# HGRN2's values projected 512 features wide and kept in the residual's place, in a four-layer trunk on one core

## The chip, the cores and the metric

The kernel runs on 1 core of one Trainium2 chip. Time is device microseconds of one launch on that core. The kernel before takes 2690.08 us, the median of 3 runs (2689.09 to 2697.81).

## The reference

The reference sends 1024 positions of 1024 features, in f32, through four layers. Each layer is `x = x + gate * mixer(rmsnorm(x, norm_g) * (1 + scale) + shift)`, with shift, scale and gate from a conditioning vector, and every mixer ends in `(o * silu(z)) @ w_out`. Layers 0 and 3 are HGRN2, layer 1 is sliding-window attention, layer 2 is gated DeltaNet. Cut to what the change touches, they are:

```python
# HGRN2, 8 heads of 128, chunks of 64 (layers 0 and 3)
q, f_pre, i_, z = split(h @ w_in, 4)          # i_ holds the values, 1024 features
f = lb + (1 - lb) * sigmoid(f_pre);  k = (1 - lb) * sigmoid(-f_pre);  q = silu(q)
A = einsum('bhtd,bhsd,bhtsd->bhts', q_, k_, dec)
o = A @ v_ + (q_ * exp(b)) @ S                # then S is carried on
o = rmsnorm(o, onorm_g);  y = (o * silu(z)) @ w_out

# sliding-window attention, 16 query heads on 4 key heads of 64 (layer 1)
q = rope(rmsnorm(q)); k = rope(rmsnorm(k)); p = softmax(s with a learned sink); o = p @ v

# gated DeltaNet, 16 value heads of 128, chunks of 64 (layer 2)
q, k, v = split(silu(causal_conv(qkv, conv_w)))     # then l2norm of q and k
X = triangular_solve(A + eye, rhs)                  # A is 64x64, strictly lower
```

## The kernel before, in words

**Tiling and stages.** The residual x lies in SBUF as two halves of 512 positions (`x[0]`, `x[1]`, 2 MB each, two slots with the tag "x"), features on the partitions. The normed input of a layer lies beside it, split into a high and a low part (`hhi`, `hlo`, four slots with the tag "h"). Every projection product is a triple on TensorE: high by high, low by high, high by low (`mm3`, L201 to L206). The weights of a projection are loaded as f32 (`w_raw`, three buffers), rounded on ScalarE (`w_hi`, L179) and subtracted on VectorE (`w_lo`, L180) by `load_w`.

There are two kinds of input projection. `proj_fm` (L509) puts the features on the partitions and streams 512 positions in one product. `proj_tm` (L1170) puts the positions on the partitions and streams 256 features: HGRN2's values, and the queries, keys and values of the attention layer. In HGRN2 it is called by `proj_v(m)` (L1013), once for each pair of heads, and the values of the pair go to a buffer `hg_v`.

**HGRN2** (L956). `mix(h, d)` (L1026) computes the scores of one head by levels of a tree over the chunk. At level 5 a burst of small products (L1087), 96, 64 and 32 columns wide, fills three partition strips of `lev_ps`. After that come the state, the products with the values, the norm, four transposes on TensorE into `ot_ps` (L1136), the product with the gate `hg_zs` on VectorE (L1139) and a DMA to DRAM (`od`, L1141). The output projection reads `od` back as `o_in` (L1192). Heads 0 to 6 go that way; head 7 stays in SBUF.

**DeltaNet** (L537). `conv` (L636) is a causal convolution: two reads of PSUM on ScalarE (`gd_xs` L644, `gd_tb` L648), three multiply-adds on VectorE (L650), a Tanh. `inverse` (L732) inverts the 64x64 blocks in four steps, each a burst of small products into `z_ps` (L811 to L836) with copies behind it. `norm_apply` (L496) makes hhi and hlo, by way of a buffer `n_t`, eight pieces for each half.

**What sets the order.** Every engine runs its instructions in the order that a scheduler gave them, from priorities. `weave` (L68) interleaves streams of work by the costs that they yield. `early` (L114) raises a projection's start, `burst` (L134) and `tied` (L138) keep the small products of one step together. All DMAs named here are issued by SyncE (SP), on one queue. `spill_x` and `fill_x` (L125, L129) send a half of x to DRAM and bring it back. Before the change that happens in layers 1 and 2 alone.

## Time and profile before

| what | value |
|---|---|
| median of 3 runs | 2690.08 us (2689.09 to 2697.81) |
| the profiled execution's own time | 2695.95 us |
| its span, first to last instruction | 2694.2 us |
| granted TensorE clock, mean | 0.992 |
| TensorE products busy | 2609.7 us, 97% |
| VectorE busy | 2010.2 us, 75% |
| ScalarE busy | 1272.9 us, 47% |
| GpSimd busy | 136.7 us, 5% |

The first row is the measure; the others come from one execution that was profiled. "Busy" is the union of an engine's instructions in time. Products follow one another before the last has ended, so the modelled length of one product (0.39 us for 512 columns) is longer than the step from one start to the next; it is the steps that add up to the span. The granted clock is a share of full speed: 1.0 is 2.4 GHz, 0.5 is 1.2 GHz. The first projection product of layer 0 starts at 55 us; layer 0 ends near 631 us, layer 1 near 1112, layer 2 near 2110, layer 3 at the end.

### The profile page before, as it was taken

The page shows a single profiled execution, that of the slowest core. Times are in us where ns is not written, and L with a number is a line of the kernel's source. Part 1 is how long each engine was busy: PE and PEld are TensorE (multiplying, and loading weights), DVE is VectorE, ACT ScalarE, POOL GpSimd, SP SyncE. Part 2 cuts the span into 40 slices and gives each one's busy share as a digit, 9 for nine tenths or more (in the row PEclk, how much of TensorE's full clock was granted, in tenths as well). Part 3 has the DMA queues.
Part 4 walks back from the last instruction along what each step waited for, and adds up shares of the span by engine and source line. Part 5 has one row for each costly group of instructions (what it writes and reads, how often), then busy time and mean ns, then how long its engine had stood idle before and what let it go on. Part 6 is the DMA issues. An engine that isn't in the chain of part 4 may idle for free.

```text
span 2694.2 us, 51458 instructions
## 1 busy us (share of the span) xinstructions
PE 2609.7 (97%) x18927; PEld 2102.4 (78%) x18927; DVE 2010.2 (75%) x5619; ACT 1272.9 (47%) x3268; POOL 136.7 (5%) x352
## 2 busy tenths in 40 slices
PE   8999999999999999999999999999999999999998
PEld 4878878778878777677877777777788878787877
DVE  6776766788687877777988888989876766656575
ACT  4333333444454655454556556666644433333342
POOL 0000100000000000001001101100000000000000
PEclk9999999999999999999999999999999999999999
DMA  6332222344223252333343333333584221111133
GB/s 241 92 93 84 68 79 72 110 137 157 59 87 103 75 158 91 114 98 84 102 115 99 96 105 100 94 97 82 179 254 132 71 60 37 56 51 43 49 118 115
DMA packets 361490, 273.29 MB, mean 101 GB/s; under 512 B 70499, under 2 KB 294166, under 8 KB 361238
## 3 DMA queue, kind: packets, MB, share of 16 engines
q1 hardware_dynamic: 360950, 268.96, 33.9%
q8 instruction: 149, 2.44, 0.4%
q14 instruction: 103, 0.84, 0.1%
q0 software_dynamic: 288, 1.05, 0.1%
HBM read 224.77 MB, written 45.15 MB: 100 GB/s over the span
## 4 chain that ended last, share of the span: by engine, by line
PE 71%; DVE 17%; DMA 5%; ACT 3%; issue 3%; SPq 1%; POOL 0%; DVEq 0%; ACTq 0%; POOLq 0%
PE proj_ps L206 10%; PE proj_ps L205 9%; PE proj_ps L204 9%; PE outp_ps L204 5%; PE outp_ps L205 5%; PE outp_ps L206 5%; DMA ada_w<-in_ada_w_dram 3%; PE projt_ps L204 3%; PE projt_ps L206 3%; PE projt_ps L205 3%; DVE w_lo L180 2%; DVE gd_tb L650 2%; PE pv_ps L1374 1%; DVE ada_acc L413 1%; PE w_ps L890 1%
## 5 line engine op out<-in xcount | busy, mean ns | idle before, releaser
L204 PE MATMUL proj_ps<-hhi,w_hi 128*128 128x512 f32 x1664 | 675.8, 406 | 6.1 <-ACT gd_tb L648 5.9
L206 PE MATMUL proj_ps<-hhi,w_lo 128*128 128x512 f32 x1664 | 679.9, 409 | 0.0
L205 PE MATMUL proj_ps<-hlo,w_hi 128*128 128x512 f32 x1664 | 671.2, 403 | 0.0
L204 PEld LDWEIGHTS proj_ps<-hhi,w_hi 128*128 128x128 f32 x1664 | 315.3, 190 | 59.4 <-ACT gd_tb L648 6.3
L205 PEld LDWEIGHTS proj_ps<-hlo,w_hi 128*128 128x128 f32 x1664 | 314.7, 189 | 59.0 <-issue 2.4
L206 PEld LDWEIGHTS proj_ps<-hhi,w_lo 128*128 128x128 f32 x1664 | 315.0, 189 | 56.1 <-issue 1.0
L179 ACT CAST w_hi<-w_raw 128x512 fp32r<-128x512 f32 x332 | 202.0, 611 | 303.3 <-PE proj_ps L205 188.1
L180 DVE TENSOR_TENSOR w_lo<-w_raw,w_hi 128x512 fp32r<-128x512 f32 x332 | 223.1, 674 | 155.2 <-ACT w_hi L179 129.1
L205 PE MATMUL projt_ps<-w_lo,hhi 128*128 128x256 f32 x896 | 258.7, 291 | 4.7 <-DVE w_lo L180 4.7
L204 PE MATMUL projt_ps<-w_hi,hhi 128*128 128x256 f32 x896 | 257.8, 290 | 0.6 <-ACT w_hi L179 0.6
L206 PE MATMUL projt_ps<-w_hi,hlo 128*128 128x256 f32 x896 | 256.8, 290 | 0.0
L204 PE MATMUL outp_ps<-o_hi,w_hi 128*128 128x512 f32 x576 | 229.2, 400 | 4.7 <-ACT o_hi L1200 3.4
L205 PE MATMUL outp_ps<-o_lo,w_hi 128*128 128x512 f32 x576 | 229.4, 399 | 0.0
L206 PE MATMUL outp_ps<-o_hi,w_lo 128*128 128x512 f32 x576 | 226.8, 396 | 0.7 <-DVE w_lo L183 0.7
L205 PEld LDWEIGHTS projt_ps<-w_lo,hhi 128*128 128x128 f32 x896 | 171.1, 192 | 8.1 <-DVE w_lo L180 6.0
L204 PEld LDWEIGHTS projt_ps<-w_hi,hhi 128*128 128x128 f32 x896 | 171.1, 192 | 3.7 <-ACT w_hi L179 1.0
L206 PEld LDWEIGHTS projt_ps<-w_hi,hlo 128*128 128x128 f32 x896 | 170.8, 192 | 2.4 <-issue 1.0
L650 DVE SCALAR_TENSOR_TENSOR gd_tb<-gd_xs,taps,gd_tb 128x512 f32<-128x512 f32 x192 | 145.2, 756 | 28.3 <-ACT gd_tb L648 19.7
L182 ACT ACTIVATE w_hi<-w_raw,par 128x512 fp32r<-128x512 f32 (+1 forms) x136 | 94.3, 698 | 137.0 <-PE outp_ps L205 89.2
L204 PEld LDWEIGHTS outp_ps<-o_hi,w_hi 128*128 128x128 f32 x576 | 108.8, 189 | 29.1 <-ACT o_hi L1200 4.9
L413 DVE SCALAR_TENSOR_TENSOR ada_acc<-ada_w,par,ada_acc 128x512 f32<-128x512 f32 x140 | 104.8, 749 | 33.4 <-DMA ada_w<-in_ada_w_dram 32.5
L206 PEld LDWEIGHTS outp_ps<-o_hi,w_lo 128*128 128x128 f32 x576 | 108.7, 189 | 23.5 <-DVE w_lo L183 1.3
(398 smaller groups left out, 4894.8 us busy)
## 6 DMA issues: line engine op xcount, KB each, us to landing
ada_w<-in_ada_w_dram SPq DMA_DIRECT2D x160, 256.0 KB, 2.8
w_raw<-in_hg_in_w_dram SPq DMA_DIRECT2D x136, 256.0 KB, 2.8
w_raw<-in_gd_in_w_dram SPq DMA_DIRECT2D x108, 256.0 KB, 3.0
o_in<-od SPq DMA_DIRECT2D x72, 256.0 KB, 3.2
w_raw<-in_gd_out_w_dram SPq DMA_DIRECT2D x64, 256.0 KB, 2.9
w_raw<-in_sw_in_w_dram SPq DMA_DIRECT2D x48, 256.0 KB, 2.9
w_raw<-in_hg_out_w_dram SPq DMA_DIRECT2D x40, 256.0 KB, 2.8
ada_w<-in_ada_w_dram SPq DMA_DIRECT2D x8, 1024.0 KB, 9.2
```

What stands on the lines that cost most here:

```text
L179: nc.scalar.copy(hi, raw)
L180: nc.vector.tensor_tensor(lo, raw, hi.bitcast(F32), ALU.subtract)
L182: nc.scalar.activation(hi, raw, AF.Copy, scale=scale)
L204: mm(out, a[0], b[0], start=start, stop=False)
L205: mm(out, a[0], b[1], start=False, stop=False)
L206: mm(out, a[1], b[0], start=False, stop=stop)
L413: self.nc.vector.scalar_tensor_tensor(acc, w, c, acc, ALU.mult, ALU.add)
L650: nc.vector.scalar_tensor_tensor(y, xs[:, j:j + HT], w(j), y, ALU.mult, ALU.add)
L890: nc.tensor.matmul(po[:, hd[a]], dd["u"][a, hf][:, cs], rhs, start=True, stop=True)
L1374: nc.tensor.matmul(po[a * 64:(a + 1) * 64], vg[:, n + 1 - nkb + b, :], p4[:, :, a, :], start=b == 0, stop=b == nkb - 1)
```

## The change

1. **Values.** `proj_wide` and `load_wide` project HGRN2's values 512 features wide, for four heads at a time, into `projw_ps`. The values lie in the two "x" slots (`hg_v`), those of head 7 in two small tiles. x goes to DRAM before both HGRN2 layers and comes back ahead of their output projection.
2. **HGRN2's output.** For heads 0 to 6 the four TensorE transposes are replaced by one 32x32-block transpose on VectorE and four DMAs of 64 KB to a new DRAM tile `pd`; `gate()` reads it back in the next half's level 3, multiplies by the gate and stores to `od`.
3. **Level 5.** The burst has 16 products at most 64 columns wide on four strips, and is tied; one more copy on ScalarE.
4. **DeltaNet's inverse.** The bursts into `z_ps` are issued behind the final product of the triple that was written last (`apart`), with larger yields; `ZL` hands the gate projections out in halves, so their weights are loaded twice.
5. **The norm of the second half** is a generator. In DeltaNet its pieces are issued between the convolutions of the first half, and the projection starts with k, q and three z of the first half. `n_t` lies in PSUM.
6. **Attention.** v and q of the first half come first, k of all positions after; k's reciprocal root is taken for two tiles at once; the products with the values are tied behind both transposes.
7. **The stored output** uses an "h" slot in place of a pool of its own.

```diff
-ZL = ((2, 0, 1),), ((3, 0, 1),), ((4, 0, 1),), ((5, 0, 1),), ((6, 0),), ((6, 1),), ((7, 0, 1),), ()
+ZL = ((2, 1), (3, 0)), ((3, 1), (4, 0)), ((4, 1), (5, 0)), ((5, 1), (6, 0)), ((6, 1),), ((7, 0),), ((7, 1),), ()
...
+    def apart(self, mms):
+
+        with self.tc.issue_after(self.mm.ins):
+            self.tied(mms)
...
+    def load_wide(self, w, c0, pool):
+
+        return [self.load_w(w[:, k, c0:c0 + HT], None, (None, pool)[k % 2]) for k in range(KT)]
+
...
-            t = self.np.tile([P, HT], F32, name="n_t", tag="n_t", bufs=NB["n_t"])
+            t = self.psum("lev", "n_t", 2)
             G, S = self.gcol[:, i, k:k + 1], self.shift(i, k)
             nc.vector.scalar_tensor_tensor(t, x[:, k, :], G, rb, ALU.mult, ALU.mult)
-            nc.scalar.activation(hhi[:, k, :], t, AF.Identity, bias=S)
+            self.piece = nc.scalar.activation(hhi[:, k, :], t, AF.Identity, bias=S)
             nc.vector.scalar_tensor_tensor(hlo[:, k, :], t, S, hhi[:, k, :].bitcast(F32), ALU.add, ALU.subtract)
+            yield 1
...
-            nc.scalar.copy(xs[:, 3:], ps)
+            with self.tc.issue_after(self.hold.ins) if self.hold else nullcontext():
+                nc.scalar.copy(xs[:, 3:], ps)
...
-                nc.vector.scalar_tensor_tensor(y, xs[:, j:j + HT], w(j), y, ALU.mult, ALU.add)
+                last = nc.vector.scalar_tensor_tensor(y, xs[:, j:j + HT], w(j), y, ALU.mult, ALU.add)
+
+            self.piece = None
+            with self.tc.issue_after(last.ins):
+                drain(take(self.last, self.parts))
+            self.hold = self.piece
...
-            with self.burst():
-                for g in range(N):
-                    for z, p_, b_ in ((za, 0, 1), (zb, 2, 3)):
-                        nc.tensor.matmul(z[R[b_], g, :], uv[R[p_], g, R[b_]], Tc[R[p_], g, :], start=True, stop=True)
+            self.apart([lambda g=g, z=z, p_=p_, b_=b_: nc.tensor.matmul(z[R[b_], g, :], uv[R[p_], g, R[b_]], Tc[R[p_], g, :], start=True, stop=True)
+                        for g in range(N) for z, p_, b_ in ((za, 0, 1), (zb, 2, 3))])
...
-            yield 900
+            yield 2200
...
-        self.early(proj_kq(0, ds[0], ((0,),)), EV)
+        self.parts = 4
+        self.early(chain(proj_kq(0, ds[0], ((0,),)), proj_z(1, ds[1], (0,)), proj_z(2, ds[2], (0,))), EV)
+        drain(self.last)
         self.spill_x(1)
...
-                    ds[h]["v", hf] = v[:, :, (h % 2) * P:(h % 2 + 1) * P]
+
+        vs, v7 = [None, None], [mp.tile([P, NC, P], F32, name=f"hg_v7{n}") for n in range(2)]
+
+        def proj_v(m):
+
+
+            def ev(tt, ps):
+                hf, c = divmod(tt, NC)
+                if vs[hf] is None:
+                    vs[hf] = self.xslot("hg_v").rearrange("p (c a) n -> p c (a n)", a=2)
+                n = HT - m * P
+                nc.scalar.copy(vs[hf][:, c, m * HT:m * HT + n], ps[:, :n])
+                if m:
+                    nc.scalar.copy(v7[hf][:, c, :], ps[:, n:])
+
+            yield from self.proj_wide(self.load_wide(w_in, 2 * D + m * HT, mp), ev, range(2 * NC))
+
+        value = lambda h, hf: v7[hf] if h == H - 1 else vs[hf][:, :, h * P:(h + 1) * P]
+        v4 = lambda x, o: x.rearrange(f"p ({o} r) -> p c b r", c=NC, b=4)
+        pend = []
+
+        def gate():
+
+            h, hf, z = pend.pop()
+            rows = (slice(h * P, (h + 1) * P), slice(hf * HT, (hf + 1) * HT))
+            t = tl("tmp")
+            nc.sync.dma_start(t, self.pd[rows])
+            nc.vector.tensor_tensor(v4(z, "c b"), v4(t, "b c"), v4(z, "c b"), ALU.mult)
+            nc.sync.dma_start(od[rows], z)
...
-                        with self.burst():
-                          for c in range(NC):
-                            for g in range(3):
-                                gs = slice(g * 32, (g + 1) * 32)
-                                nc.tensor.matmul(pl[gs, c, g + 1:, :], kg[:, c * P + g * 32:c * P + (g + 1) * 32], xv[:, c, g::3 if g == 0 else 4 - g, :][:, :3 - g, :] if g < 2 else xv[:, c, 2:3, :], start=True, stop=True)
-                        for g in range(3):
-                            gs = slice(g * 32, (g + 1) * 32)
-                            nc.scalar.copy(at[gs, :, (g + 1) * 32:], pl[gs, :, g + 1:, :].rearrange("p c b t -> p c (b t)"))
+
+                        def mm(c, k, g, x, b):
+                            return nc.tensor.matmul(pl[g * 32:(g + 1) * 32, c, b], kg[:, c * P + k * 32:c * P + (k + 1) * 32], xv[:, c, x, :], start=True, stop=True)
+
+                        self.tied([lambda c=c, m=m: mm(c, *m) for c in range(NC) for m in (
+                            (0, 3, slice(6, 7), slice(3, 4)), (0, 0, slice(0, 4, 3), slice(1, 3)),
+                            (1, 1, slice(1, 5, 3), slice(2, 4)), (2, 2, slice(2, 3), slice(3, 4)))])
+                        for k, g, b0, b1 in ((0, 0, 1, 3), (1, 1, 2, 4), (2, 2, 3, 4), (0, 3, 3, 4)):
+                            nc.scalar.copy(at[k * 32:(k + 1) * 32, :, b0 * 32:b1 * 32], pl[g * 32:(g + 1) * 32, :, b0:b1, :].rearrange("p c b t -> p c (b t)"))
                         yield 900
+                    if l == 3 and pend:
+                        gate()
...
-                yield 436
-                of = tl("tmp")
-                nc.vector.tensor_tensor(of, pt, d["zs", hf], ALU.mult)
                 if h < HA:
-                    nc.sync.dma_start(od[h * P:(h + 1) * P, hf * HT:(hf + 1) * HT], of)
+
+
+                    nc.vector.tensor_tensor(v4(on, "b c"), v4(po, "c b"), r[:, :, None, None].to_broadcast([P, NC, 4, 32]), ALU.mult)
+                    ob = tl("tmp")
+                    nc.vector.transpose(ob, on)
+                    dst = self.pd[h * P:(h + 1) * P, hf * HT:(hf + 1) * HT].rearrange("(b q) (a t) -> a q b t", b=4, a=4)
+                    for a in range(4):
+                        nc.sync.dma_start(dst[a], ob[a * 32:(a + 1) * 32].rearrange("q (b t) -> q b t", b=4))
+                    pend.append((h, hf, d["zs", hf]))
...
         ds = [dict() for _ in range(H)]
+        drain(self.last)
         gv = proj_v(0)
-        self.early(chain(proj(0, ds[0], "qf", (0,)), take(gv, 8)))
+        self.early(chain(proj(0, ds[0], "qf", (0,)), take(gv, 16)))
+        self.spill_x(1)
         drain(chain(gv, proj(0, ds[0], "qf", (1,))))
         for h in range(H - 1):
             ns = 18 if h == 0 else NS[0]
-            if h % 2 == 0:
-                g = chain(proj(h, ds[h], "z"), proj(h + 1, ds[h + 1], "qfz"))
-            else:
-                g = chain(proj(h + 1, ds[h + 1], "qf"), proj_v((h + 1) // 2))
-            weave(self.tc, (mix(h, ds[h]), 16000, 0, 1, PRH), (g, 41600, 0, 1, 0), (take(side, ns), ns, 0, 1, 0))
+            gs = {0: [(0, "z")], 1: [], H - 2: [(h, "z"), (h + 1, "qfz")]}.get(h, [(h, "z")])
+            if h < H - 2:
+                gs.append((h + 1, "qfz" if h == 0 else "qf"))
+            g, tot = chain(*[proj(x, ds[x], p) for x, p in gs]), 10400 * sum(len(p) for _, p in gs)
+            if h == 1:
+                g, tot = chain(g, proj_v(1)), tot + 41600
+            weave(self.tc, (mix(h, ds[h]), 16000, 0, 1, PRH), (g, tot, 0, 1, 0), (take(side, ns), ns, 0, 1, 0))
         drain(side)
+        for hf in range(2):
+            self.fill_x(hf)
...
+
+    def proj_wide(self, ws, evac, tts):
+
+        for tt in tts:
+            ps = self.proj_ps("projw_ps")
+            hf, ts = tt // 4, slice((tt % 4) * P, (tt % 4 + 1) * P)
+            for k in range(KT):
+                self.mm3(ps, (self.hhi[hf][:, k, ts], self.hlo[hf][:, k, ts]), ws[k], k == 0, k == KT - 1)
+                if k % 2:
+                    yield 1300
+            evac(tt, ps)
...
+        def proj_v(hf):
+            return self.proj_tm(self.load_tm(w_in, 1280), ev_v, (2 * hf, 2 * hf + 1))
+
+        ds = [dict(q=[None, None], zs=[None, None], rq=[None, None]) for _ in range(G)]
+        drain(self.last)
+        self.early(chain(proj_v(0), proj_q(0, ds[0], (0, 1))))
         self.spill_x(1)
-        drain(kv(1))
-        ds = [dict() for _ in range(G)]
-        drain(proj(0, ds[0]))
+        drain(proj_v(1))
+        drain(self.proj_tm(self.load_tm(w_in, 1024), ev_k))
+        drain(chain(proj_z(0, ds[0]), proj_q(0, ds[0], (2, 3))))
...
-        k.norm_apply(layers[0], 0, rb)
-        rb = k.norm_stats(1, k.load_x(sp, 1))
-        k.norm_apply(layers[0], 1, rb)
-        if layers[0] % 3:
-            k.spill_x(0)
+        drain(k.norm_apply(layers[0], 0, rb))
+        k.last = k.norm_apply(layers[0], 1, k.norm_stats(1, k.load_x(sp, 1)))
+        drain(k.last)
+        k.spill_x(0)
...
-                k.norm(nxt, hf)
-                if nxt % 3 and hf == 0:
+                a = k.norm_apply(nxt, hf, k.norm_stats(hf))
+                if hf == 0:
+                    drain(a)
                     k.spill_x(0)
-                if hf == 1:
+                else:
+                    k.last = a
                     k.nst.close()
```

Order on ScalarE at the start of DeltaNet, before: `hhi` are the pieces of the norm, `w_hi` the rounded weights, `gd_xs` and `gd_tb` the reads of the first projection's PSUM.

```order
L179 CAST w_hi<-w_raw 128x512
L505 ACTIVATE hhi<-n_t,mod 128x512 x2
L179 CAST w_hi<-w_raw 128x512
L505 ACTIVATE hhi<-n_t,mod 128x512 x2
L644 COPY gd_xs<-proj_ps 128x512
L648 ACTIVATE gd_tb<-proj_ps,taps 128x512
L644 COPY gd_xs<-proj_ps 128x512
L555 CAST gd_wab<-w_raw 128x8x32
L592 ACTIVATE gd_tmp<-gd_tmp 128x16
L651 ACTIVATE gd_tb<-gd_tb 128x512
L678 COPY gd_kt<-ktr_ps 128x512
```

The same place after; line numbers have moved (L514 is the old L505, L186 L179, L655 L644, L659 L648; `n_sq` is a square for the norm's statistics).

```order
L490 ACTIVATE n_sq<-x_10967 128x512
L186 CAST w_hi<-w_raw 128x512
L655 COPY gd_xs<-proj_ps 128x512
L659 ACTIVATE gd_tb<-proj_ps,taps 128x512
L565 CAST gd_wab<-w_raw 128x8x32
L186 CAST w_hi<-w_raw 128x512 x2
L667 ACTIVATE gd_tb<-gd_tb 128x512
L514 ACTIVATE hhi<-n_t,mod 128x512 x2
L186 CAST w_hi<-w_raw 128x512
L602 ACTIVATE gd_tmp<-gd_tmp 128x16
L694 COPY gd_kt<-ktr_ps 128x512
```

All pieces of the second half's norm stood ahead of the first convolution's reads; now the reads stand first and the pieces come by pairs behind them.

Order on SP at the start of layer 0, before: `x_in` are the inputs of the second half, the `128x2x256` loads the values' weights, the `128x4x128` loads those of q, f and z.

```order
L177 DMA w_raw<-in_hg_in_w_dram 128x2x256
L395 DMA ada_w_383<-in_ada_w_dram 128x4x512
L177 DMA w_raw<-in_hg_in_w_dram 128x2x256 x2
L304 DMA x_in<-in_x_dram 128x1024 x4
L263 DMA taps_in<-in_gd_conv_w_dram 128x128
L177 DMA w_raw<-in_hg_in_w_dram 128x2x256
L177 DMA w_raw<-in_hg_in_w_dram 128x4x128 x6
```

The same place after; `128x512` are the wide weights of the values, `xd<-x_136` and `xd<-x_438` the two halves of x on their way to DRAM.

```order
L184 DMA w_raw<-in_hg_in_w_dram 128x512 x3
L315 DMA x_in<-in_x_dram 128x1024 x4
L129 DMA xd<-x_136 128x8x512
L274 DMA taps_in<-in_gd_conv_w_dram 128x128
L129 DMA xd<-x_438 128x8x512
L184 DMA w_raw<-in_hg_in_w_dram 128x512 x5
L184 DMA w_raw<-in_hg_in_w_dram 128x4x128 x6
```

Both stores of x stand ahead of five of the eight wide weights. Before, no store of x stood here.

Order on SP at the end of layer 0, before: the last stores of `od`, weights for the next layer's modulation (`ada_w`), weights of the output projection, loads of `o_in`.

```order
L1141 DMA od_76<-hg_tmp 128x512
L427 DMA ada_w<-in_ada_w_dram 128x512 x6
L177 DMA w_raw<-in_hg_out_w_dram 128x4x128
L177 DMA w_raw<-in_hg_out_w_dram 128x3x128
L177 DMA w_raw<-in_hg_out_w_dram 128x4x128
L1141 DMA od_76<-hg_tmp 128x512
L177 DMA w_raw<-in_hg_out_w_dram 128x3x128
L177 DMA w_raw<-in_hg_out_w_dram 128x4x128
L177 DMA w_raw<-in_hg_out_w_dram 128x3x128
L1192 DMA o_in<-od_76 128x512 x3
```

The same place after; `x_5673<-xd` brings the first half of x back.

```order
L1057 DMA od_76<-hg_zs 128x512
L438 DMA ada_w<-in_ada_w_dram 128x512 x3
L134 DMA x_5673<-xd 128x8x512
L1176 DMA pd<-hg_tmp 32x4x128 x4
L438 DMA ada_w<-in_ada_w_dram 128x512
L184 DMA w_raw<-in_hg_out_w_dram 128x4x128
L184 DMA w_raw<-in_hg_out_w_dram 128x3x128
L184 DMA w_raw<-in_hg_out_w_dram 128x4x128
L184 DMA w_raw<-in_hg_out_w_dram 128x3x128
L184 DMA w_raw<-in_hg_out_w_dram 128x4x128
L184 DMA w_raw<-in_hg_out_w_dram 128x3x128
L1253 DMA o_in<-od_76 128x512 x3
```

The load of x's first half stands ahead of the last head's stores to `pd` and of all weights of the output projection.

## Rows read from the trace of the kernel before

**Rows 1.** The page's first part, the whole span.

```profile
span 2694.2 us, 51458 instructions
PE 2609.7 (97%) x18927; PEld 2102.4 (78%) x18927; DVE 2010.2 (75%) x5619; ACT 1272.9 (47%) x3268; POOL 136.7 (5%) x352
```

**Rows 2.** The page's chain that ended last, by engine.

```profile
PE 71%; DVE 17%; DMA 5%; ACT 3%; issue 3%; SPq 1%; POOL 0%; DVEq 0%; ACTq 0%; POOLq 0%
```

**Rows 3.** Windows: PE, PEld, DVE, ACT, POOL busy; clock, DMA share, GB/s.

```profile
1100.00:1150.00 50.00, 43.43 (x183) 32.45 (x181) 38.42 (x66) 23.12 (x49) 2.92 (x10) 0.93 0.40 118
...
1250.00:1300.00 50.00, 48.40 (x365) 39.06 (x355) 34.08 (x90) 27.58 (x95) 2.82 (x6) 0.90 0.25 67
1300.00:1350.00 50.00, 50.00 (x240) 39.89 (x238) 47.82 (x153) 29.39 (x99) 2.33 (x12) 1.00 0.39 105
```

**Rows 4.** Timeline of TensorE, 256-column products: start us, length us, what.

```profile
341.99 0.28 PE L205 MATMUL projt_ps<-w_lo,hhi 128*128 128x256 f32 x1
342.11 0.28 PE L206 MATMUL projt_ps<-w_hi,hlo 128*128 128x256 f32 x1
```

**Rows 5.** Timeline of TensorE, 512-column products.

```profile
99.66 0.39 PE L204 MATMUL proj_ps<-hhi,w_hi 128*128 128x512 f32 x1
99.89 0.40 PE L205 MATMUL proj_ps<-hlo,w_hi 128*128 128x512 f32 x1
```

**Rows 6.** Timeline of TensorE around one set of transposes, layer 0.

```profile
542.97 0.39 PE L204 MATMUL outp_ps<-o_hi,w_hi 128*128 128x512 f32 x1
543.33 0.63 PE L1136 MATMUL ot_ps<-ident,hg_tmp 128*128 128x128 f32 x4
543.72 0.48 PE L205 MATMUL outp_ps<-o_lo,w_hi 128*128 128x512 f32 x1
```

**Rows 7.** Lines by form: busy us, mean ns | idle before, releaser.

```profile
L859 DVE STREAM_TRANSPOSE gd_of<-gd_of 128x512 f32<-128x512 f32 x32 | 22.5, 704 | 0.1
...
L1198 DVE TENSOR_TENSOR o_z<-o_in,o_z 128x512 f32<-128x512 f32 x32 | 21.8, 687 | 9.6 <-DMA o_z<-zd 6.6 <-issue 1.4 <-DMA o_in<-od 1.2
...
L1136 PE MATMUL ot_ps<-ident,hg_tmp 128*128 128x128 f32 x128 | 20.8, 280 | 5.9 <-DVE hg_tmp L1132 5.6
```

**Rows 8.** Timeline of TensorE around one burst of level 5.

```profile
207.26 0.85 PE L1087 MATMUL lev_ps<-hg_X,hg_kg 128*32 128x96 f32 x24
208.04 0.39 PE L205 MATMUL projt_ps<-w_lo,hhi 128*128 128x256 f32 x1
```

**Rows 9.** Tile `z_ps`, who waited for it: us in all, times.

```profile
  PE z_ps L828: 6.6, 7
```

**Rows 10.** Waits, 1110 to 1180 us: us in all, times, longest.

```profile
PE proj_ps L204 <- ACT gd_tb L648: 5.9, 1, 5.9
```

**Rows 11.** Chain of work that ended last, 1128 to 1140 us.

```profile
1136.67 0.60 ACT gd_tb L648
...
1138.53 0.43 PE proj_ps L206
1138.96 0.43 PE proj_ps L204
```

**Rows 12.** Waits, 640 to 700 us.

```profile
PE projt_ps L205 <- DVE w_lo L180: 4.2, 4, 1.4
```

**Rows 13.** Timeline of SP's queue, start of layer 1.

```profile
660.53 0.37 SPq L132 DMA_DIRECT2D x<-xd x1
661.13 35.53 SPq L177 DMA_DIRECT2D w_raw<-in_sw_in_w_dram x11
```

**Rows 14.** DMA issues: count, KB each, median us to landing.

```profile
xd<-x SPq DMA_DIRECT2D x4, 2048.0 KB, 8.0
x<-xd SPq DMA_DIRECT2D x4, 2048.0 KB, 8.4
```

**Rows 15.** Timeline of SP's queue, start of layer 0.

```profile
50.62 0.42 SPq L263 DMA_DIRECT2D taps_in<-in_gd_conv_w_dram x1
```

**Rows 16.** Timeline of TensorE, first projection product.

```profile
55.11 0.50 PE L204 MATMUL proj_ps<-hhi,w_hi 128*128 128x512 f32 x1
```

More of the change, by code (lines that the diff above doesn't have):

```diff
@@ L1 @@
 import math
-from contextlib import ExitStack
+from contextlib import ExitStack, nullcontext
 import numpy as np
@@ L205, in mm3 @@
         mm(out, a[0], b[1], start=False, stop=False)
-        mm(out, a[1], b[0], start=False, stop=stop)
+        self.mm = mm(out, a[1], b[0], start=False, stop=stop)
     def setup(self, tmp):
@@ L815, in inverse @@
                 nc.gpsimd.tensor_copy(uv[R[b], :, R[b]], Uc[R[b]])
-            yield 900
+            yield 2200
             za, zb = bank("z_ps", 32), bank("z_ps", 32)
-            self.tied([f for g in range(N) for f in (
+            self.apart([f for g in range(N) for f in (
                 lambda g=g: nc.tensor.matmul(zb[R[2], g, :], Z[R[3], g, 0:32], Uc[R[3], g, :], start=True, stop=True),
@@ L833, in inverse @@
             nc.vector.tensor_copy(Z[up, 8:16], z[lo])
-            yield 900
+            yield 2200
             z = bank("z_ps", 64)
-            self.tied([lambda g=g, q=q: nc.tensor.matmul(z[q, g % 8, :], Z[up, g, :], uv[up, g, up], start=True, stop=True)
+            self.apart([lambda g=g, q=q: nc.tensor.matmul(z[q, g % 8, :], Z[up, g, :], uv[up, g, up], start=True, stop=True)
                        for n in range(8) for g, q in ((n + 8, up), (n, lo))])
```

146 lines of the change are left out of this document (72 added, 74 removed).

## The prediction

> **What bounds the kernel now.** I read the page's busy times first, then the chain that ended last, then windows of 50 us, then the waits, and at last single products in the timeline. Busy times [rows 1]: TensorE's products cover 2609.7 of 2694.2 us, so only 84.5 us in the whole span have no product in flight. The next engine, VectorE, has 2010.2. The chain [rows 2] says the same: 71% of it is TensorE, then 17% VectorE. So an edit is worth what it takes out of TensorE's stream of products, or out of those 84.5 us. The windows [rows 3] show where the stream is thin: at DeltaNet's start (1100 to 1150) products cover 43.43 of 50 us and the granted clock is 0.93; in the first inverse (1250 to 1300) 48.40 at 0.90; right behind it products cover all 50.00, and there VectorE is busy for 47.82. What one product costs is the step from one start to the next: 0.12 us for 256 columns [rows 4], 0.23 us for 512 [rows 5].
>
> **The change part by part.** The sum is made against the profiled execution's own 2695.95 us (span 2694.2) and then put on the median of 2690.08, which is 5.9 lower.
>
> *Wide values.* One layer's values are 4 pairs of heads x 8 position tiles x 8 slices x 3 = 768 products of 256 columns; both HGRN2 layers have 1536, and the change makes 768 of 512. 1536 x 0.12 = 184.3 us against 768 x 0.23 = 176.6: **-8**. The steps are read to 0.01 us, so the ends are -2 and -12. The copies on ScalarE keep their total size and weight loads their number.
>
> The Trainium skill (TensorE: Matmul & The Clock Gate, section Back-to-back issue gap) has a table for a product by itself: 262 cycles for 256 columns, 518 for 512. By it one wide product costs nearly two narrow ones, at 2.4 GHz an estimated 167.4 us against 165.9, and the sum would come out 6 us later. This trace's steps are longer at both widths, with 0.01 us per product that the wide form saves; the measured steps are used.
>
> *Output transposes.* Around one set, the step from the product ahead to the product behind is 543.72 - 542.97 = 0.75 us, of which 0.23 is that product's own: 0.52 for four transposes [rows 6]. 28 of 32 sets go (heads 0 to 6, two halves, two layers): 28 x 0.52 = 14.6. TensorE also stood 5.9 us ahead of the 32 sets, waiting for VectorE [rows 7], 5.2 for 28. I take all of the first and half of the second, since a stall that goes lets the next burst meet its own: **-17**, ends -12 and -20. What replaces them is off TensorE: 28 block transposes of 0.704 us on VectorE [rows 7], small stores and loads on SP's queue with half a head's time to land. VectorE has room there: 75% over the span [rows 1].
>
> *Level 5.* One burst of 12 products sets TensorE back by 208.04 - 207.26 = 0.78 us [rows 8]. There are 32 (8 heads, 2 halves, 2 layers). The new one has 16 products and the same columns in all (192 a chunk); the widest strip falls from 96 to 64. If the widest strip counts, 0.78 becomes 0.52 and 8 us go; if columns count, nothing; if the number counts, it is 1.04 and 8 us come. I take **-3**, between the first two; ends -8 and +8. The added copy on ScalarE is hidden: that engine is at 47% [rows 1].
>
> *Fewer breaks.* In the written order the projection's stream is interrupted 1028 times before and 933 after; 28 of the 95 are the transposes counted above. A break costs the step to the first small product, 0.36 in place of 0.23, so 0.13 [rows 6]: 67 x 0.13 = 8.7 at most. Some of the missing ones are bursts that merely meet each other: **-4**, ends 0 and -9.
>
> *The inverse's bursts.* TensorE waited 6.6 us in 7 waits before the third burst, for copies of the second [rows 9]; the thin stretch at clock 0.90 loses 0.10 x 50 = 5 us more [rows 3]. In the new order inverses 3 to 7 have 14 to 18 products between bursts instead of 2 to 10; the first two keep 4 to 10, and the last has hardly any projection left between its bursts, which may cost 2. **-4**, ends 0 and -12.
>
> *DeltaNet's start.* TensorE waits 5.9 us once [rows 10], because ScalarE does all norm pieces of the second half ahead of `gd_xs` and `gd_tb`; and when it resumes, products step by 1138.96 - 1138.53 = 0.43 us, near twice 0.23 [rows 11]. The window's clock of 0.93 is 3.5 us [rows 3], so 9.4 in all. The reads now stand ahead of the pieces, and about 169 products (39 us at 0.23) of the first half stand ahead of the next join, against about 91 before. What is late next is VectorE, which does three multiply-adds and then four pieces before the next convolution. **-8**, ends -4 and -10.
>
> *Attention's start.* 4.2 us of waiting for `w_lo` [rows 12]. With v and q first and k's root for two tiles, VectorE and ScalarE have less ahead of the weights: **-3**, ends 0 and -5.
>
> *x to DRAM and back.* Four stores more at 8.0 us and four loads at 8.4 [rows 14]; SP's queue takes them in line with the weights. At layer 0's start SP is free of other work at 51.0 [rows 15], the first product starts at 55.1 [rows 16], and two groups of 24 products (11 us) come ahead of the values. So the values start at 66.2 and need their fourth wide weight at 68.3; it is issued behind two stores of 8.0, at 67 or later, and must land and be rounded. That makes some 3 us for the fourth, and less for each after it: **+5**, ends 0 and +11. At the ends of layers 0 and 3 a load of 8.4 stands ahead of the output weights; some 84 products (19 us) still run between the last use of the values and the first output product, which is its cover; without it each end costs 8.4: **+2** each, ends 0 and +8. Layer 3's start has the output projection before it as cover: **+1**, ends 0 and +8.
>
> *VectorE and ScalarE in DeltaNet.* Half-wise gate projections load 24 weights twice: 24 more subtractions of 128x512, at the 0.687 us of such an operation [rows 7] 16.5 us, where VectorE already has 47.82 of 50 [rows 3]. Most fall between convolutions: **+3**, ends 0 and +17. The stored output in an "h" slot and the tied attention products I put at nothing: the first moves only buffers, and the second trades two breaks for one wait of the same copies.
>
> Sum: -8 -17 -3 -4 -4 -8 -3 = -47, and +5 +2 +2 +1 +3 = +13: **-34 us**. 2695.95 - 34 = 2662 for a profiled execution, 2656 on the median.
>
> **The rivals.** *More than that (about 2622).* All gains at their far ends are -76; with +8 of costs that is -68. For it: the small pauses are many, and the new order spaces the bursts everywhere. Against it: the gains share causes, and a stream with fewer pauses meets VectorE sooner, which is nearly full in DeltaNet [rows 3].
>
> *Hardly anything (about 2684).* The wide product gives its lower end (2), level 5 nothing, the 16.5 us of VectorE in DeltaNet all land on the path, and layer 0 starts 11 us late: -34 + 6 + 3 + 13.5 + 6 = -5.5. This is also the case in which the change does not do what it says: bursts that stand apart in the order meet the same waits, because VectorE, not the order, is late.
>
> *Slower (about 2712).* The eight added transfers land on the path: 4 x 8.0 + 4 x 8.4 = 65.6 us [rows 14], of which 10 are in the sum, so 56 more. It decides once about 52 of the 65.6 are exposed (2656 + 42 is the bound of slower). For it: at the start of attention a load of x stands ahead of weights in the same queue [rows 13], and TensorE's waits for `w_lo` lie right behind it. Against it: these waits are 4.2 us in all [rows 12], half of one transfer.
>
> The Trainium skill (DMA: Bandwidth & Descriptors, section Two DMAs through the same engine are not ordered) says that within one queue of one DMA engine descriptors start in order. By that a weight behind 2 MB of x can't overtake it, which speaks for this rival wherever a weight is needed soon; the trace agrees with 35.53 us for eleven weight issues behind the load [rows 13].
>
> **How the numbers follow.** The forecast, 2640 to 2672 around 2656: 0.60. More: 0.17. Hardly anything, 2672 to 2698: 0.17. Slower: 0.06. 0.3% of 2690 is 8 us, about what a measurement of this kernel can tell from no change, so faster means below 2682: 0.60 + 0.17 + half of 0.17 = 0.86; the other half, 0.08, is no change; slower 0.06. The range 2616 to 2686 leaves out the slower case, the upper part of the third and a little below: some 0.14.
>
> **What would show it.** Products `projw_ps` step by 0.23 and `ot_ps` has 16 products in place of 128. The bursts of level 5 step by under 0.78. The wait of 5.9 at DeltaNet's start is gone and that stretch has a clock above 0.93. `z_ps` L828's wait falls well under 6.6. At the start of layer 0 a gap before `projw_ps` of about 5 us, with a weight as releaser. I am wrong if the gaps behind loads and stores of x sum to more than 20 us, or if VectorE's waits in DeltaNet grow by what TensorE saves.

## The result, and the profile after

The changed kernel takes 2702.46 us (2699.55 to 2710.01, 7 runs) against 2690.08 before: a ratio of 1.0043, 95% interval 1.0028 to 1.0058. The forecast was 2656, 34 us faster; it is 12 us slower, a miss of 46 us. The profiled execution has a span of 2701.9 us and took 2703.65.

The changed kernel's page, first part (answers to [rows 1]):

```profile
span 2701.9 us, 50651 instructions
PE 2586.2 (96%) x18303; PEld 2052.7 (76%) x18303; DVE 2023.2 (75%) x5649; ACT 1283.4 (47%) x3340; POOL 147.0 (5%) x352
```

TensorE's products cover 23.5 us less than before, as they should with fewer of them; but the span without any product grew from 84.5 to 115.7 us. So work was saved and waits ate it. Where they are is read from the start of the second half's norm statistics (`n_ps`), the one mark that each layer's end has. The changed kernel, timeline of TensorE at the ends of layers 0, 1 and 2:

```profile
627.33 1.02 PE L494 MATMUL n_ps<-ones,n_acc 128*128 128x1 f32 x8
...
1110.42 0.95 PE L494 MATMUL n_ps<-ones,n_acc 128*128 128x1 f32 x8
...
2131.15 0.58 PE L494 MATMUL n_ps<-ones,n_acc 128*128 128x1 f32 x4
```

The kernel before, the same marks:

```profile
638.91 1.02 PE L486 MATMUL n_ps<-ones,n_acc 128*128 128x1 f32 x8 [0.34 <-DVE n_acc L483]
...
1117.83 1.05 PE L486 MATMUL n_ps<-ones,n_acc 128*128 128x1 f32 x8 [0.43 <-DVE n_acc L483]
...
2122.80 0.58 PE L486 MATMUL n_ps<-ones,n_acc 128*128 128x1 f32 x4
```

Layer 0 ends 11.6 us earlier. Layer 1 takes 483.1 instead of 478.9 us; in the profiles of the experiments below, none of which edits layer 1, it takes 476.4 (e6) to 483.9 us (e4), so these 4 us are not clear of noise. DeltaNet takes 1020.7 instead of 1005.0, 16 us lost. Layer 3, to the end of the span, takes 570.8 instead of 571.4, although it has the same edits as layer 0.

**DeltaNet.** Windows of the changed kernel (PE, PEld, DVE, ACT, POOL busy; clock, DMA share, GB/s), where [rows 3] had 43.43 at 0.93 and 48.40 at 0.90:

```profile
1100.00:1150.00 50.00, 43.54 (x174) 33.76 (x173) 37.07 (x65) 23.36 (x55) 2.07 (x10) 0.90 0.43 127
...
1250.00:1300.00 50.00, 47.78 (x442) 39.00 (x441) 39.91 (x100) 30.40 (x99) 6.73 (x12) 1.00 0.45 117
...
1900.00:1950.00 50.00, 33.47 (x333) 26.30 (x331) 30.53 (x68) 22.90 (x63) 3.61 (x6) 0.73 0.66 197
```

The kernel before, the last of these windows:

```profile
1900.00:1950.00 50.00, 45.48 (x407) 35.02 (x406) 40.66 (x89) 32.52 (x90) 5.64 (x8) 0.97 0.66 207
```

The start is no better: 43.54 us covered, at a clock of 0.90. TensorE's waits there, 1110 to 1200 us (us in all, times, longest), have a new first row in place of the 5.9 us of [rows 10]:

```profile
PE proj_ps L217 <- DVE w_lo L187: 4.8, 3, 2.2
PE proj_ps L215 <- ACT gd_tb L659: 1.6, 1, 1.6
```

Near 1900 us there is a new hole: 12 us less covered and a clock of 0.73. The waits of the changed kernel there, 1895 to 1940 us:

```profile
PE vtr_ps L674 <- DVE gd_tb L668: 7.2, 1, 7.2
...
PE z_ps L824 <- ACT gd_Tc L809: 5.9, 1, 5.9
```

Both belong to the last unit. `vtr_ps` turns its values; `z_ps` is the first burst of the last inverse, which waits for blocks that have just come back from DRAM. Before, products of the projection ran there. The first of an inverse's four bursts, shown by the tile `z_ps`, tells when the first and the last inverse ran (min, median, max ns of one product; first to last start). The kernel before:

```profile
L811 PE MATMUL z_ps<-gd_Tc,gd_uq x512: 191/191/212, 1247.0 to 1904.8; 32*32 32x32 f32 x171
```

The changed kernel:

```profile
L824 PE MATMUL z_ps<-gd_Tc,gd_uq x512: 191/191/255, 1268.6 to 1919.6; 32*32 32x32 f32 x171
```

From the layer's mark, the first inverse begins at 1268.6 - 1110.4 = 158.2 us, before at 1247.0 - 1117.8 = 129.2: the row of eight inverses, which the written order puts one after another, starts 29 us later. Products of `proj_ps` from the mark to that point, the changed kernel and then the kernel before:

```profile
1110.42:1268.60 158.18, 132.39 (x535) 101.62 (x534) 6.81 (x10) 20.75 (x34) 0.97 0.41 111
```

```profile
1117.83:1247.00 129.17, 102.95 (x425) 80.04 (x425) 5.37 (x8) 16.73 (x28) 0.97 0.38 104
```

The 110 products more, at 0.23 us, are 25 of the 29 us. The projection itself does not end later. Its last products from 1850 us on, the changed kernel and then the kernel before:

```profile
L217 PE MATMUL proj_ps<-hhi,w_lo x48: 389/397/582, 1850.4 to 1903.3; 128*128 128x512 f32 x48
```

```profile
L206 PE MATMUL proj_ps<-hhi,w_lo x61: 387/397/586, 1850.2 to 1918.6; 128*128 128x512 f32 x61
```

Before, projection products still ran when the first burst of the last inverse was over (1904.8). Now the last of them starts at 1903.3, and that burst ends its starts at 1919.6, with nothing of the projection beside it.

**Layer 3.** The waits of the changed kernel, 2340 to 2590 us, have a row that before has not:

```profile
PE o_ps L1152 <- POOL hg_at L1115: 8.6, 5, 1.8
```

Timeline of GpSimd around the first of the five: the four copies of one step together, and then the last of the four alone.

```profile
2384.18 5.09 POOL L1115 COPY hg_at<-hg_A 32x128 f32<-32x128 f32 x4 [75.97 <-DVE hg_A L1110]
```

```profile
2386.01 3.26 POOL L1115 COPY hg_at<-hg_A 32x128 f32<-32x128 f32 x1
```

Timeline of VectorE beside it:

```profile
2386.29 0.55 DVE L1133 TENSOR_TENSOR hg_kg<-hg_kg,hg_F 128x384 f32<-128x384 f32 x1
2386.76 0.41 DVE L1005 TENSOR_TENSOR hg_kg<-hg_k,hg_f 128x256 f32<-128x256 f32 x1
...
2388.10 0.68 DVE L187 TENSOR_TENSOR w_lo<-w_raw,w_hi 128x512 fp32r<-128x512 f32 x1
2388.70 0.41 DVE L1096 TENSOR_TENSOR hg_X<-hg_qf,hg_F 128x256 f32<-128x256 f32 x1
2390.76 0.29 DVE L1159 COPY hg_S<-s_ps 128x128 f32<-128x128 f32 x1 [1.65 <-PE s_ps L1156]
```

The kernel before, GpSimd at the same step of the layer, together and the last alone:

```profile
2384.81 1.68 POOL L1081 COPY hg_at<-hg_A 32x128 f32<-32x128 f32 x4 [35.34 <-DVE hg_A L1076]
```

```profile
2386.20 0.29 POOL L1081 COPY hg_at<-hg_A 32x128 f32<-32x128 f32 x1
```

Four small copies take 5.09 us instead of 1.68, and nearly all of the difference is one of them, 3.26 against 0.29. It ends at 2389.27, 0.16 us after the last of seven VectorE operations in a row, each on two tensors in SBUF and each started before the one ahead had ended. The Trainium skill (GPSIMD Engine Reference, section Specifications) says that GpSimd shares its SBUF interfaces with VectorE, with contention where a VectorE instruction has two SBUF inputs; the trace agrees in that the held-up copy lies beside such operations. That condition alone does not tell which copy is held up: in the kernel before, too, VectorE is busy with operations on two SBUF inputs for 1.53 of the 1.68 us, smaller ones among them. What lets a copy in between two operations was not tested.

**What came as forecast.** Level 5 is cheaper: a burst, once it has started, sets TensorE back by 229.72 - 229.14 = 0.58 us, against 0.78 in [rows 8]; all bursts that lie between products of a projection, with no wait behind them, show the same two numbers. The wide products step by 0.23 us. Timeline of TensorE, changed kernel:

```profile
228.23 0.39 PE L215 MATMUL projw_ps<-w_hi,hhi 128*128 128x512 f32 x1
228.46 0.40 PE L216 MATMUL projw_ps<-w_lo,hhi 128*128 128x512 f32 x1
229.14 0.65 PE L1119 MATMUL lev_ps<-hg_X,hg_kg 128*32 128x32 f32 x32 [0.28 <-DVE hg_F L1130]
229.72 0.50 PE L217 MATMUL projw_ps<-w_hi,hlo 128*128 128x512 f32 x1
```

The wait of the inverse's third burst fell from 6.6 us in [rows 9] to 3.1 (`z_ps`, who waited for it), and the window from 1250 to 1300 us above has a clock of 1.00 instead of 0.90:

```profile
  PE z_ps L842: 3.1, 3
```

The stores of x at layer 0's start cost nothing: from 48 to 80 us TensorE waits 0.2 us for a weight of the values.

```profile
PE projw_ps L215 <- ACT w_hi L186: 0.2, 1, 0.2
```

**A wait that no run takes out.** From 520 to 640 us, at the end of layer 0, the output projection waits for VectorE's subtraction of its weights; the kernel before has 0.7 us of it, and all runs below that start from the changed kernel have 4.3 to 5.6. Its cause was not tested.

```profile
PE outp_ps L217 <- DVE w_lo L190: 5.2, 2, 4.0
```

### The profile page after: what moved, and what is told of

It reads as the page before. It is cut to its first block, busy times and chain, and to the rows that moved or that the text cites. A ratio compares the mean times of both kernels' runs of the same rounds, so it can differ in the third digit from the quotient of the medians.

```text
span 2701.9 us, 50651 instructions
## 1 busy us (share of the span) xinstructions
PE 2586.2 (96%) x18303; PEld 2052.7 (76%) x18303; DVE 2023.2 (75%) x5649; ACT 1283.4 (47%) x3340; POOL 147.0 (5%) x352
## 4 chain that ended last, share of the span: by engine, by line
PE 68%; DVE 15%; DMA 8%; ACT 4%; issue 2%; SPq 1%; POOL 1%; DVEq 0%; ACTq 0%; POOLq 0%
PE proj_ps L217 9%; PE proj_ps L215 9%; PE proj_ps L216 9%; PE outp_ps L216 5%; PE outp_ps L215 5%; PE outp_ps L217 5%; DMA ada_w<-in_ada_w_dram 2%; PE projw_ps L215 2%; PE projw_ps L216 2%; PE projw_ps L217 2%; DVE w_lo L187 2%; DVE gd_tb L661 1%; PE projt_ps L216 1%; PE projt_ps L217 1%; PE projt_ps L215 1%
## 5 line engine op out<-in xcount | busy, mean ns | idle before, releaser
L187 DVE TENSOR_TENSOR w_lo<-w_raw,w_hi 128x512 fp32r<-128x512 f32 x356 | 238.9, 675 | 174.9 <-ACT w_hi L186 172.8
L186 ACT CAST w_hi<-w_raw 128x512 fp32r<-128x512 f32 x356 | 216.8, 612 | 274.0 <-PE proj_ps L216 155.0
L216 PEld LDWEIGHTS outp_ps<-o_lo,w_hi 128*128 128x128 f32 x576 | 110.2, 191 | 24.4 <-DVE o_lo L1262 2.0
L190 DVE SCALAR_TENSOR_TENSOR w_lo<-w_raw,par,w_hi 128x512 fp32r<-128x512 f32 (+1 forms) x136 | 96.7, 715 | 40.2 <-ACT w_hi L189 38.4
L1115 POOL COPY hg_at<-hg_A 32x128 f32<-32x128 f32 x128 | 68.8, 537 | 1003.9 <-DVE hg_A L1110 504.8
L216 PE MATMUL projt_ps<-w_lo,hhi 128*128 128x256 f32 x384 | 111.3, 292 | 2.5 <-DVE w_lo L187 2.5
L215 PE MATMUL projt_ps<-w_hi,hhi 128*128 128x256 f32 x384 | 111.1, 292 | 2.0 <-ACT w_hi L186 2.0
L217 PE MATMUL projt_ps<-w_hi,hlo 128*128 128x256 f32 x384 | 111.4, 292 | 0.0
```

What stands on the lines that cost most here:

```text
L186: nc.scalar.copy(hi, raw)
L187: nc.vector.tensor_tensor(lo, raw, hi.bitcast(F32), ALU.subtract)
L190: nc.vector.scalar_tensor_tensor(lo, raw, scale, hi.bitcast(F32), ALU.mult, ALU.subtract)
L215: mm(out, a[0], b[0], start=start, stop=False)
L216: mm(out, a[0], b[1], start=False, stop=False)
L217: self.mm = mm(out, a[1], b[0], start=False, stop=stop)
```

## The experiments

Each was timed in five rounds against the kernel before on the same chip; the ratio of the changed kernel is 1.0043. The experiments ran on three chips, so runs are compared by their ratios; differences of medians are given as round numbers.

**e1: cover for the last inverse.**

```diff
-ZL = ((2, 1), (3, 0)), ((3, 1), (4, 0)), ((4, 1), (5, 0)), ((5, 1), (6, 0)), ((6, 1),), ((7, 0),), ((7, 1),), ()
+ZL = ((2, 1),), ((3, 0, 1),), ((4, 0, 1),), ((5, 0, 1),), ((6, 0),), ((6, 1),), ((7, 0, 1),), ()
```

> The changed kernel with the gate projections handed out as before from unit 1 on, so that both halves of unit 7's gate (96 products of 512 columns, 22 us) lie beside the last inverse again instead of one half (48 products, 11 us). Theory A (the last inverse has lost its cover): the stretch of half clock near 1906 to 1934 us goes, TensorE's waits of 7.2 and 5.9 us before vtr_ps and z_ps shrink below 3, and the time falls by 12 to 20 us from 2702 to 2682 to 2690. Theory B (the load of x ahead of the last inverse's own loads is what makes it late, cover or not): the load of x still stands between the store tblk and its loads, the waits stay above 8 us in all, and the time falls by under 6 us.

2692.83 us, 1.0009 (0.9999 to 1.0019): 9 us better, under Theory A's 12 to 20 and above B's 6. Waits at the last inverse, 1885 to 1935 us:

```profile
PE z_ps L842 <- DVE gd_uq L837: 2.0, 1, 2.0
PE z_ps L850 <- DVE gd_Z L847: 1.5, 1, 1.5
PE z_ps L824 <- ACT gd_Tc L809: 1.1, 1, 1.1
...
PE vtr_ps L674 <- DVE gd_tb L668: 0.3, 1, 0.3
```

7.2 and 5.9 became 0.3 and 1.1, with the load of x where it was. The cover was missing; but it is not the whole of it: the first inverse still begins 158 us behind the layer's mark. The edit also spares VectorE 16 subtractions of weights; between the first inverse and these waits, though, TensorE waits 17.6 us here and 16.3 in the changed kernel, so what is saved does not show there.

**e2: the load of x.** In the changed order it stands between the store of the last inverse's blocks and their loads; here it is issued behind them.

```diff
...
-                self.fill_x(0)
+                with self.tc.issue_after(self.tload.ins):
+                    self.fill_x(0)
```

> The changed kernel with one order on SP's queue turned back: the load of x's first half (2 MB) at the end of DeltaNet is issued behind the loads of the last inverse's blocks from tblk, as before, not between the store and these loads. Theory B: the blocks land 6 to 8 us earlier, z_ps waits under 1 us for gd_Tc, the stretch at half clock shrinks from 27 to under 14 us, and the time falls by 9 to 14 us, to 2688 to 2693. Theory A: VectorE has the blocks late anyway (it ends gd_Tb at 1902, against 1892 before) and there are no products left by then, so the time falls by under 5 us.

2705.3 us, 1.0057 (1.0045 to 1.0069): not faster. The blocks' loads took 4.04 us to issue instead of 9.69 and `z_ps` waited 1.8 us for them, but the wait before stayed; waits from 1890 to 1940 us:

```profile
PE vtr_ps L674 <- DVE gd_tb L668: 7.2, 1, 7.2
```

Theory B's 9 to 14 us do not come. From the layer's mark, the last inverse's first burst is over 3 us sooner than in the changed kernel, but from there to the layer's end it takes 219.2 us instead of 211.6. Whether the load of x, now later, costs these 8 us was not followed, so the run does not show that its place is worth nothing.

**e3: the copies on ScalarE.**

```diff
-                            nc.gpsimd.tensor_copy(at[gs, :, gs], A[gs].rearrange("p (c t) -> p c t", c=NC))
+                            nc.scalar.copy(at[gs, :, gs], A[gs].rearrange("p (c t) -> p c t", c=NC))
```

> The changed kernel with the four copies per head and half from hg_A to hg_at on ScalarE instead of GpSimd. Theory C (GpSimd's copies are held up by VectorE's back-to-back operations in layer 3: 5.09 us for four copies where others take 1.6): TensorE's five waits of 1.6 to 1.8 us before o_ps in layer 3 go, the clock there stays at 1.0, and the time falls by 8 to 12 us, to 2690 to 2694. Rival: hg_A itself is late, because VectorE finishes it late; then the waits stay with ScalarE as releaser, and the time is within 3 us of 2702.

2688.43 us, 0.9993 (0.9984 to 1.0001): 14 us better, a little more than expected. The five waits are gone: from 2120 to 2580 us products wait 0.6 us in all for `hg_at`, for ScalarE. So `hg_A` was not late, its copies were.

**e4: values 256 wide again.**

```diff
-            for k in range(KT):
-                self.mm3(ps, (self.hhi[hf][:, k, ts], self.hlo[hf][:, k, ts]), ws[k], k == 0, k == KT - 1)
-                if k % 2:
-                    yield 1300
+            for n in range(2):
+                ns = slice(n * 256, (n + 1) * 256)
+                for k in range(KT):
+                    self.mm3(ps[:, ns], (self.hhi[hf][:, k, ts], self.hlo[hf][:, k, ts]), [w[:, ns] for w in ws[k]], k == 0, k == KT - 1)
+                    if k % 4 == 3:
+                        yield 1300
```

> The changed kernel with HGRN2's values projected 256 features wide again, two products for each wide one, into the same place, from the same weights and in the same order. If a product costs what its step says (0.12 and 0.23 us), the 1536 narrow products take 8 to 10 us more than the 768 wide ones: 2710 to 2713. If width is worth nothing beside the other waits: within 3 us of 2702.

2705.75 us, 1.0055 (1.0042 to 1.0068): 3 us slower, with an interval that overlaps the changed kernel's. By the two intervals the width that gave the change its name is worth between nothing and some 8 us.

**e5: e1 and e3 together.**

> Both edits that helped: the gate projections handed out as before from unit 1 on, and the copies from hg_A to hg_at on ScalarE. They act in different layers (DeltaNet's last unit; HGRN2, mostly layer 3). If they are independent, 9 and 14 us add up: 2677 to 2682, faster than both kernels. If they share a cause (a VectorE that is late in general), less: 2684 to 2689.

2679.27 us, 0.9960 (0.9948 to 0.9972): the two add up.

**e6: output transposes on TensorE again,** in `mix`, with the old product and store in place of the way through `pd`.

```diff
-                if h < HA:
+                if h < 0:
...
+                    if h < HA:
+                        nc.sync.dma_start(od[h * P:(h + 1) * P, hf * HT:(hf + 1) * HT], of)
...
```

> The changed kernel with the output of heads 0 to 6 turned on TensorE again (four transposes, product with the gate, store), without the block transposes on VectorE and the way through pd. If the transposes were worth what the prediction says, the time rises by 12 to 20 us from 2702, to 2714 to 2722. If the replacement costs as much elsewhere (VectorE's 28 operations of 0.7 us and their stores), it stays within 4 us of 2702 or falls.

2711.93 us, 1.0076 (1.0064 to 1.0088): 9 us slower, half of the 17 of the forecast and below the 12 that were expected at least. In this kernel the held-up copies sit in layer 0 instead; waits from 300 to 480 us:

```profile
PE o_ps L1152 <- POOL hg_at L1115: 7.0, 4, 2.0
```

and layer 3 has none. So an edit that shifts VectorE can bring this wait in or take it out, and the block transposes, which this kernel does not have, are not needed for it. By the two profiles layer 0 is 14.7 us longer than in the changed kernel, with some 6 us more of this wait, and layer 3 2.8 us shorter, with 8.6 less. An estimate from these figures, without the waits: 9 + 6 = 15 us for the transposes, near the 17. No run has e6 together with e3, which would settle it.

**e7: DeltaNet's start as before in the source,** on top of e1. With the early gates gone, they are handed out as in the kernel before.

```diff
...
-        self.parts = 4
-        self.early(chain(proj_kq(0, ds[0], ((0,),)), proj_z(1, ds[1], (0,)), proj_z(2, ds[2], (0,))), EV)
         drain(self.last)
+        self.early(proj_kq(0, ds[0], ((0,),)), EV)
...
```

> As e1 (2693), and DeltaNet's start as before: all pieces of the second half's norm ahead, only k, q and one gate projection of the first half early, the other gates handed out as before. If the new start gives the 8 us that the prediction took for it, this is 5 to 10 us slower than e1: 2698 to 2703. If the stall only moved from the convolution's reads to w_lo behind VectorE, it is within 4 us of 2693, or faster.

2676.43 us, 0.9942 (0.9927 to 0.9957): not slower but some 16 us faster than e1. The stall of [rows 10] is not there, although no piece of the norm is interleaved. Window at the start, and ScalarE's first read of the projection and its first piece of the norm:

```profile
1100.00:1150.00 50.00, 49.06 (x224) 37.18 (x222) 43.10 (x92) 26.99 (x62) 2.41 (x11) 1.00 0.45 133
```

```profile
1107.35 0.59 ACT L655 COPY gd_xs<-proj_ps 128x512 f32<-128x512 f32 x1 [2.29 <-PE proj_ps L217]
...
1112.12 0.69 ACT L514 ACTIVATE hhi<-n_t,mod 128x512 fp32r<-128x512 f32 x1 [0.53 <-DVE n_t L513]
```

In the kernel before the pieces stood ahead of that read; here the read is ahead of them. Which other part of the change brings that about, `n_t` in PSUM for one, was not tested.

**e8: the inverse's bursts as before.** `apart` becomes `tied` (the first burst a plain `burst`), the costs go back.

```diff
-            yield 2200
+            yield 900
...
-                st_.append((inverse(u + 1, ds[u + 1]), 34300, 0, 1, PR[1]))
+                st_.append((inverse(u + 1, ds[u + 1]), 28000, 0, 1, PR[1]))
```

> The changed kernel with the four bursts of the inverse issued as before (raised priority, not behind the last triple) and with the smaller costs for the interleaving (900 and 1300, 28000 in all). If the spacing gives the 4 us of the prediction, this is 3 to 8 us slower than 2702: 2705 to 2710. Rival: the larger costs stretch the inverse, so that the last one ends after the projections have run out; then this is 5 to 12 us faster, 2690 to 2697, and the waits before vtr_ps and z_ps near 1905 us shrink.

2693.83 us, 1.0012 (1.0002 to 1.0022): some 9 us faster, as the rival has it. The last first-step burst is over at 1911.1 instead of 1919.6, and the waits before `vtr_ps` and `z_ps` shrink from 7.2 and 5.9 to 6.0 and 3.5 us. The run turns back the place of the bursts and their costs together, so it does not tell the two apart.

**e9 and e10: the helpful edits together,** e7 with e3, and in e9 the bursts of e8 too.

> e7 (DeltaNet's start and hand-out of gates as before, 2676) with the copies to hg_A's target on ScalarE and the inverse's bursts as before. Theory (the chain of eight inverses sets DeltaNet's end, GpSimd's held-up copies cost layer 3): 13 us for the copies and 4 to 8 for the bursts come off, 2655 to 2660. Rival: once the chain starts early the spacing of the bursts pays, as the prediction had it; then this is above e10 by 3 us or more.

> e7 with the copies on ScalarE, the bursts spaced as in the changed kernel: 2660 to 2666 if the 13 us of the copies add to e7's 2676.

e9: 2668.92 us, 0.9920 (0.9904 to 0.9937), above the 2655 to 2660 that were expected. e10: 2664.95 us, 0.9908 (0.9896 to 0.9921), as expected, the fastest of all and 24 us faster than the kernel before on the same chip (2689.28). With the chain early, the spaced bursts no longer cost; whether they gain is not settled, the intervals overlap.

**e11: the copies on ScalarE in the kernel before.**

> The kernel before, with only the copies from hg_A to hg_at on ScalarE. In its trace no product waits for GpSimd there and four copies take 1.6 to 2.4 us. Theory (the change brought this wait in): within 4 us of 2690. Rival (GpSimd is slow there in any case, and the copies are always on the path): 8 to 14 us faster.

2686.28 us, 0.9988 (0.9979 to 0.9997): 3 us. So most of e3's 14 us is a wait that the change brought in.

**e12: only the early gates out** and handed out as in the kernel before, the norm's pieces still between the convolutions.

```diff
...
-        self.early(chain(proj_kq(0, ds[0], ((0,),)), proj_z(1, ds[1], (0,)), proj_z(2, ds[2], (0,))), EV)
+        self.early(chain(proj_kq(0, ds[0], ((0,),))), EV)
...
```

> As e7, but with the norm's pieces of the second half still issued four at a time behind the convolutions; only the two early gates are taken out of the start and the gates are handed out as before. If the early gates alone delay the chain of inverses, this is as fast as e7, 2672 to 2680, and the first inverse begins near 121 us after the start as there. If the interleaving also costs, it is 4 to 10 us slower than e7.

2675.33 us, 0.9944 (0.9932 to 0.9956), as e7. Its window at the start, and its `z_ps`:

```profile
1100.00:1150.00 50.00, 47.33 (x216) 36.04 (x215) 42.01 (x82) 25.99 (x60) 2.07 (x10) 1.00 0.44 130
```

```profile
L824 PE MATMUL z_ps<-gd_Tc,gd_uq x512: 190/191/212, 1233.0 to 1884.7; 32*32 32x32 f32 x171
```

The first inverse begins at 1233.0 - 1109.5 = 123.5 us, with 433 products of `proj_ps` in front of it. The early gates and their half-wise hand-out together cost 27 us (2702.46 - 2675.33): the hand-out, which e1 turns back by itself, some 10, and the early place some 17 (2692.83 - 2675.33). The interleaved norm is harmless, and without the early gates the start is nearly full, 47.33 of 50 at clock 1.00. But so it is in e7, without the interleaving: that part of the change is not what fills it.

## Why the prediction was wrong

**DeltaNet's start (-8) is the step that failed, with the wrong sign: the new start costs some 17 us (e7 and e12 against e1).** I counted the stall that the new order removes, and took the 169 products ahead of the next join as cover. They are work ahead of the first inverse, and the eight inverses follow one another through the layer. 110 products more in front, at 0.23 us, are 25 of the 29 us by which the first inverse started later, and at the other end the projection ran out 16 us before the first burst of the last inverse was over, where before it had lasted 14 us longer than that burst. The stall was the right thing to remove: without the early gates it is gone, and the first inverse begins 123.5 us behind the mark instead of 129.2. With them TensorE waited for `w_lo` instead (4.8 us, 1110 to 1200 us), behind a VectorE that the prediction had named as next in line and not priced. e12 has the same norm pieces and convolutions and 0.5 us of that wait, so it goes with the early gates.

**The cover of the last inverse** was seen and mis-sized: the prediction says that the last one "has hardly any projection left between its bursts, which may cost 2". The half-wise hand-out that leaves it so costs some 10 us (e1), where the term for it (+3) counted VectorE's subtractions alone.

**The inverse's bursts (-4)** did what the term counted, 3.1 us of waiting instead of 6.6 and a clock of 1.00 instead of 0.90, and still lost: e8 gains 9 us by undoing them. I take it that the larger costs stretch a row of inverses that was already late; the run does not separate them from the spacing. With the row started early (e9, e10) nothing of this loss is left.

**A wait that is no term of the sum** is that of the products for GpSimd's copies. The prediction put what came to VectorE at nothing, because that engine has room on average; it did not see that GpSimd has to get its copies between VectorE's operations. The wait costs some 14 us in the changed kernel (e3), 9 to 11 on top of e7 (e10), and at most some 3 in the kernel before (e11). Which part of the change brings it in is open.

**Output transposes (-17)** were right in mechanism; what they are worth is not settled. The time says 9 (e6), but the wait for the copies moved from layer 3 to layer 0 in that run, and without it the two layers give an estimated 15.

**Wide values (-8)** came to 3, not separable from 0 (e4). The step per product was right; what 768 saved steps of 0.01 us leave at the end of the span is at the limit of what five rounds can tell. The 2 us that the prediction works out from the table of the Trainium skill (TensorE: Matmul & The Clock Gate, section Back-to-back issue gap) lie nearer than the forecast's 8, which is at the edge of the interval.

**Level 5 (-3)** was too small: 32 bursts x (0.78 - 0.58) = 6 us by their steps, near the case in which the widest strip counts; no run takes it out by itself. The stores of x at layer 0's start were put at +5 and show 0.2 us of waiting. The rival of exposed transfers did not occur; slower came from a mechanism that was not on the list. For that rival the prediction read too much into [rows 13]: of the 35.53 us of eleven weight issues, SP spent 19.1 waiting for VectorE's subtractions (`w_lo`) and 6.3 for weights to land, so they do not measure the load of x in front. The terms for attention's start and for the number of breaks were not tested apart.

The early gates with their hand-out (27 us) and the held-up copies (9 to 11 on top) make some 37 of the 46 us; e10, without both, stands at 2665, 9 above the forecast and inside its range of 2640 to 2672. That does not bear out the sum: e10 lacks the early start, and several of the other terms missed in either direction. e1, e7 and e8 overlap with the first of the two and are not added.

## What to carry to other kernels

Before a work item is moved to an early place, look for the longest row of dependent or ordered steps that starts behind it, and count what will lie beside the last step of that row; cover spent at the front is missing at the back. A free share of 25% on an engine did not tell whether a neighbour can get between its operations: read that neighbour's durations, not its share. And in this kernel, whose main engine is 97% busy, an order was worth more than a cheaper product: the edit that named the change moved some 3 us, the early place of 96 products 17, and with their hand-out 27.

## What was not expected of the hardware

One GpSimd copy of 32x128 elements stretched from 0.29 to 3.26 us beside VectorE operations on two SBUF inputs, at a VectorE share of 36 of 50 us in that stretch. It ends 0.16 us after a row of such operations, and VectorE then pauses for 1.65 us. The pause is not needed. In layer 0 of the changed kernel another copy is held up, and it ends 0.16 us after the last operation on two inputs, while VectorE goes straight on with one on a single tensor. The eight traces of changed kernels that have these copies on GpSimd show 43 copies of over 2 us; all of them end 0.15 to 0.16 us after a two-input operation, and in 11 of them VectorE goes on without a pause. The kernel before has none over 0.78 us. The copy in layer 0, GpSimd and then VectorE:

```profile
176.79 2.79 POOL L1115 COPY hg_at<-hg_A 32x128 f32<-32x128 f32 x1
```

```profile
179.02 0.41 DVE L1081 TENSOR_TENSOR hg_F<-hg_f 128x256 f32<-128x256 f32 x1
179.35 0.52 DVE L422 TENSOR_SCALAR ada_acc<-ada_w,par 128x512 f32<-128x512 f32 x1
```

Moved to ScalarE, the copies cost nothing that could be seen. The changed kernel's window with the first held-up copy, and the same stretch of layer 3 in e10, whose layer 3 starts 29 us earlier:

```profile
2350.00:2400.00 50.00, 47.79 (x467) 37.86 (x466) 35.75 (x133) 18.57 (x52) 6.40 (x8) 1.00 0.22 64
```

```profile
2321.00:2371.00 50.00, 49.59 (x478) 39.34 (x477) 37.25 (x138) 22.25 (x63) 0.00 (x0) 1.00 0.22 65
```
